# Sixty-four latent blocks of a projection: both parts of the input in one 512-column product

## Chip, cores, metric

One core of a Trainium2 chip. The metric is the device time of one execution in microseconds (us); the time before is the median of three runs. TensorE is called PE, VectorE DVE, ScalarE ACT; SyncE (SP) issues the DMAs.

## What is computed

One layer of a diffusion backbone over 256 latent tokens (`x`) and 256 context tokens, 2048 channels, in fp32. Norm and adaLN give `hn`; one input projection gives seven parts, of which a convolution branch and a recurrent branch use six:

```python
u = hn @ w_in[l] + b_in[l]
a, g, z_c, xr, z_r, gc, gr = jnp.split(u, SPLITS, axis=-1)
v = a * jax.nn.sigmoid(g)                       # conformer_branch
v = depthwise_conv(vr, p["conv_dw"], half, half)  # 31 taps, rows of 64 tokens
v = jax.nn.silu(layernorm(v + p["conv_dw_b"], p["conv_ln_g"], p["conv_ln_b"]))
y_conv = (v * jax.nn.silu(z_c)) @ p["w_conv_out"]
y_rnn = ((hf + hb) * jax.nn.silu(z_r)) @ p["w_rnn_out"]   # hf, hb: scans over xr
y = jax.nn.sigmoid(gc) * y_conv + jax.nn.sigmoid(gr) * y_rnn
x = x + gt[:, None] * (y @ p["w_o"])            # then the final RMSNorm
```

## The kernel before

Channels lie on the partitions, tokens in the free dimension. Every fp32 operand of a product is an exact pair of parts, a leading one and a remainder: the input as `xh` and `xl` (16 channel tiles, context and latents), the weights as `whi` and `wlo`. A product of the pairs is three products: `whi` with `xh`, `whi` with `xl`, `wlo` with `xh`.

After a start phase (adaLN, norms, eight xr blocks) the weights come as a stream of blocks, 128 output channels by 2048 input channels, 1 MB each. `slot` (L573) does one block: it issues the load of block s+3, and for each half of the block `block_mms` (L381) emits 24 products; then `stage_split` (L372) emits ACT's `whi` (L180) for half a block two blocks ahead and DVE's `wlo` (L185) for the half before that; then `run_deferred` (L406) runs what was put off by a number of half slots with `defer`, and `run_side` (L411) side work. For latents alone a product has 256 columns and a block is 48 products.

Side work stands in one queue: pieces with a cost in us that is written beside them (0.37 for a convolution tap). Each half slot takes pieces off the queue until half the block's budget is used up (`BUD_ZR`, `BUD_R`, `BUD`, `BUD_LN`, L26). So the program order of DVE and ACT is fixed when the program is built, and by these numbers; engines run in that order.

The order of the blocks: xr and zr in turn (zr has 16), then a and g in turn (32), zc (16), gr (16), rnn_out (16), gc (16), conv_out (16), then the output projection (w_o) in four column chunks with 512-column products. The side queue has first the recurrent branch (taps, gates on PE, scan); when it is empty, `feed` (L701) opens the memory of the second phase, and the convolution's taps come in (`conv_ops`, L647) as pairs of tiles are ready. Behind the last taps comes the LayerNorm: mean (`ln_mean`, L711), centring and squares, variance (`ln_var`, L738), `ln_rstd` (L742) and then in the side queue `ln_a` (L766: scaling on DVE, swish on ACT), `ln_b` (L770: product with the gate) and `ln_split` (L773: a leading part on ACT, a remainder on DVE), tile by tile. The sums over partitions go through PE: `ln_total` (L715) emits a product named `tot` where the program stands. Behind the last gc block everything left in the side queue is emitted at once:

```python
    while side or any(queue):
        run_side(1e9)
        run_deferred()
```

The conv_out blocks read what `ln_split` wrote. `gt_start`, the last piece of the side queue, starts a row of 64 DVE steps for adaLN's gate of the output (`gt_step`, L817), two after each gc and conv_out block and one after each half block of w_o; a chunk of 16 steps ends in a product `gps` (L833) and an ACT copy, which the evacuation of the chunk (`evac_o`, L890) needs.

Evacuation before: ACT reads the 256 columns of a block out of PSUM with bias and function in one operation (`evac_a` L688, `evac_g` L692, zc at L790; `evac_zr` L556 with two).

Of the kernel before, what the change touches and what calls it, by code (L numbers as in the profile page):

```python
# [81 lines left out]
def block_kernel(ctx, tc, xcat, xtok, fgrow, par, wada, wgt, bgt, wearly, wall, wgate, out):  # L82
# [120 lines left out]
    def ada_mms(acc, raw, rnd, n):  # L203
        # raw holds 8 // n channel tiles of 128 n columns of w_ada
# [7 lines left out]
    def ada_fin(row, part, k0, n):  # L212
        # sums of the four partial rows, channels to partitions
# [11 lines left out]
    def stat_mm(acc, x, i):  # L225
        # mean over channels: four column groups of the array take every fourth tile
# [10 lines left out]
    with ExitStack() as st:  # L237
# [28 lines left out]
        # with the tokens on the partitions, and back  # L266
# [18 lines left out]
        def normalise(ks):  # L285
# [16 lines left out]
            # partial sums, in the end where the input's first tiles were  # L302
# [69 lines left out]
    def stage_split(s, h):  # L372
        """the weights' leading parts; the remainders of the half block before"""
# [23 lines left out]
    side = deque()  # L397
# [626 lines left out]
```

## Time and profile before

| what | us |
|---|---|
| median of three runs (1145.42 to 1146.89) | 1146.66 |
| span of the profiled execution (its own time beside the runs isn't given apart) | 1142.0 |
| PE busy | 1121.5 |
| DVE busy | 924.9 |
| ACT busy | 615.1 |

The span goes from the first to the last instruction that the profile shows; a run's time has a few us more around it. Busy times overlap between engines, so they don't add up to the span. In the chain of waits every us of the span is put down to one engine: the one that the end was waiting for. A matmul's duration in the profile contains its pipeline; what one costs in a row is the distance from start to start.

### The profile page before, as it was taken

To read this page: it belongs to the slowest core of one execution; us is meant where nothing else is said; L and a number is where in the kernel's file an instruction comes from. 1 tells how busy PE (TensorE), PEld (TensorE's weight loads), DVE (VectorE), ACT (ScalarE), POOL (GpSimd) and SP (SyncE) were. 2 spreads that over 40 slices of the span, in tenths; PEclk is the share of its full clock that TensorE was granted. 3 is DMA by queue.
4 is the path that set the end of the run, shared out by engine and by line. 5 is a ranking of instruction groups with operands and counts; after the bars stand their busy time and mean duration, and the time that the engine had idled before them with its cause. 6 is when DMAs were issued, how large, how long until landed. Compare 5 with 4: busy or idle time off the path is not lost.

```text
span 1142.0 us, 20720 instructions
## 1 busy us (share of the span) xinstructions
PE 1121.5 (98%) x8316; PEld 1010.7 (88%) x8316; DVE 924.9 (81%) x1528; ACT 615.1 (54%) x838; POOL 0.2 (0%) x4
## 2 busy tenths in 40 slices
PE   6999999999999999999999999999999999999996
PEld 3777778777798989999999999999999999999885
DVE  5555588789879888899998989999985977888885
ACT  3222279777888877644454444443335854444443
POOL 0000000000000000000000000000000000000000
PEclk9999999999999999999999999999999999999999
DMA  9998444233346555465555555555554569888772
GB/s 376 400 409 324 189 134 134 102 125 125 106 141 196 160 167 164 143 209 184 185 185 171 183 183 185 175 183 178 181 188 150 169 205 324 316 310 285 268 279 93
DMA packets 67635, 233.70 MB, mean 205 GB/s; under 512 B 7505, under 2 KB 11729, under 8 KB 67153
## 3 DMA queue, kind: packets, MB, share of 16 engines
q1 hardware_dynamic: 67538, 232.37, 59.5%
q8 instruction: 65, 1.06, 0.4%
q14 instruction: 32, 0.26, 0.1%
HBM read 230.25 MB, written 2.10 MB: 203 GB/s over the span
## 4 chain that ended last, share of the span: by engine, by line
PE 98%; DVE 1%; DMA 0%; ACT 0%; issue 0%; ACTq 0%; SPq 0%; DVEq 0%
PE acc L234 72%; PE o L912 8%; PE xr L234 6%; PE gate L472 5%; PE ada L209 2%; PE part L234 2%; PE ms L228 1%; DMA hbuf<-in_xcat_dram 0%; PE tp L216 0%; PE mps L228 0%; PE gps L833 0%; PE vps L228 0%; DVE sq L259 0%; DVE wlo L171 0%; PE tot L279 0%
## 5 line engine op out<-in xcount | busy, mean ns | idle before, releaser
L234 PE MATMUL acc<-xh,whi 128*128 128x256 f32 (+1 forms) x2176 | 566.8, 296 | 0.0
L234 PE MATMUL acc<-xl,whi 128*128 128x256 f32 (+1 forms) x2176 | 552.3, 289 | 0.0
L180 ACT ACTIVATE whi<-raw 128x1024 fp32r<-128x1024 f32 x304 | 321.1, 1058 | 351.0 <-PE acc L234 277.3
L234 PEld LDWEIGHTS acc<-xh,whi 128*128 128x128 f32 x2176 | 416.7, 192 | 17.8 <-issue 9.3
L234 PEld LDWEIGHTS acc<-xl,whi 128*128 128x128 f32 x2176 | 416.9, 192 | 12.5 <-issue 7.7
L185 DVE TENSOR_TENSOR wlo<-raw,whi 128x1024 fp32r<-128x1024 f32 x304 | 371.0, 1223 | 70.0 <-ACT whi L180 66.3
L234 PE MATMUL acc<-xh,wlo 128*128 128x256 f32 (+1 forms) x2176 | 319.0, 289 | 0.0
L234 PEld LDWEIGHTS acc<-xh,wlo 128*128 128x128 f32 x2176 | 288.2, 192 | 5.0
L660 DVE SCALAR_TENSOR_TENSOR cv<-hbuf,pt,cv 128x196 f32<-128x196 f32 (+14 forms) x480 | 185.9, 451 | 13.0 <-ACT cv L651 12.6
L461 DVE SCALAR_TENSOR_TENSOR xc<-xr,pt,xc 128x510 f32<-128x510 f32 (+2 forms) x96 | 71.0, 742 | 0.2
L472 PE MATMUL gate<-xc,gw 128*128 128x512 f32 x128 | 60.0, 592 | 0.0
L820 DVE SCALAR_TENSOR_TENSOR zc<-gtraw,csil,zc 128x512 f32<-128x512 f32 x64 | 47.9, 748 | 5.4 <-DMA gtraw<-in_wgt_dram 4.7
L234 PE MATMUL xr<-xh,whi 128*128 128x512 f32 x96 | 40.4, 421 | 0.4 <-ACT xh L170 0.4
L912 PE MATMUL o<-whi,xh 128*128 128x512 f32 x128 | 40.6, 399 | 0.0
L498 DVE TENSOR_TENSOR_SCAN tr<-a,ti 128x512 f32<-128x512 f32 x32 | 39.1, 1223 | 0.7
L333 ACT ACTIVATE row<-ada 128x128 f32<-128x128 f32 (+1 forms) x22 | 7.2, 326 | 60.2 <-PE ada L209 60.2
L912 PE MATMUL o<-whi,xl 128*128 128x512 f32 x128 | 39.5, 389 | 0.0
L912 PE MATMUL o<-wlo,xh 128*128 128x512 f32 x128 | 39.4, 389 | 0.0
L234 PE MATMUL xr<-xl,whi 128*128 128x512 f32 x96 | 37.7, 392 | 0.2 <-DVE xl L171 0.2
L472 PEld LDWEIGHTS gate<-xc,gw 128*128 128x128 f32 x128 | 22.8, 189 | 17.0 <-issue 13.9
L234 PE MATMUL xr<-xh,wlo 128*128 128x512 f32 x96 | 37.4, 390 | 0.0
L209 PE MATMUL ada<-adaraw,csil 128*32 128x128 f32 (+1 forms) x704 | 32.5, 324 | 1.1 <-DVE sh L218 0.9
(169 smaller groups left out, 838.1 us busy)
## 6 DMA issues: line engine op xcount, KB each, us to landing
raw<-in_wall_dram SPq DMA_DIRECT2D x304, 512.0 KB, 3.5
adaraw<-in_wada_dram SPq DMA_DIRECT2D x64, 512.0 KB, 8.5
gtraw<-in_wgt_dram SPq DMA_DIRECT2D x32, 512.0 KB, 3.9
raw<-in_wearly_dram SPq DMA_DIRECT2D x16, 512.0 KB, 9.9
gw<-in_wgate_dram SPq DMA_DIRECT2D x32, 128.0 KB, 3.2
hbuf<-in_xcat_dram SPq DMA_DIRECT2D x2, 1024.0 KB, 7.1
cv<-in_xtok_dram SPq DMA_DIRECT2D x4, 512.0 KB, 5.8
out_dram<-cv SPq DMA_DIRECT2D x6, 256.0 KB, 2.6
```

What stands on the lines that cost most here:

```text
L180: A.activation(out=hi, in_=raw, func=AF.Copy)
L185: V.tensor_tensor(out=lo, in0=raw, in1=hi.bitcast(F32), op=SUB)
L209: PE.matmul(out=acc[g:g + 32, :w], lhsT=csil[:, k, :], rhs=raw[:, w * q:w * q + w], start=(k < 4), stop=(k >= KT - 4), tile_position=(0, g))
L228: PE.matmul(out=acc[32 * q:32 * q + 32, :], lhsT=ones[:, :32], rhs=x, start=(i < 4), stop=(i >= KT - 4), tile_position=(0, 32 * q))
L234: PE.matmul(out=acc, lhsT=w, rhs=x, start=(first and i == 0), stop=(last and i == n - 1))
L333: A.activation(out=row, in_=acc, func=AF.Copy)
L461: V.scalar_tensor_tensor(out=o, in0=i, scalar=w, in1=o, op0=MUL, op1=ADD)
L472: PE.matmul(out=acc, lhsT=u["gw"][:, c:c + 128], rhs=u["xc"], start=True, stop=True)
L498: V.tensor_tensor_scan(out=r(u["tr"]), data0=r(u["a"]), data1=r(u["ti"]), initial=0.0, op0=MUL, op1=ADD)
L660: V.scalar_tensor_tensor(out=o, in0=i, scalar=hdw[:, m * CW + j:m * CW + j + 1], in1=o, op0=MUL, op1=ADD)
L820: V.scalar_tensor_tensor(out=gt_chunk(c), in0=gt_raw[0][:, 512 * (k % 2):512 * (k % 2) + 512], scalar=csil[:, k, 0:1], in1=gt_chunk(c), op ...
L912: PE.matmul(out=acc, lhsT=y[:, k, 1, P * i:P * i + P], rhs=w[:, 512 * kk:512 * kk + 512], start=(k == 0 and w is hi and y is xh), stop=(k ...
```

## The change

The two parts of the input become one tile `xx`, in which the leading part and the remainder of a channel tile's latents lie side by side, 512 columns. In the 64 blocks zr, a, g and zc a half block is now eight products of `whi` with 512 columns, the leading part's sum in the first half of a PSUM bank and the remainder's in the second, and eight products of `wlo` with `xh` into the first half. ACT copies the second half with the bias, and half a slot later DVE adds the first half (`gather`); the function (Tanh, Silu) is an ACT operation from SBUF another half slot later, and products that follow come later still. Blocks that read the context half or come after zc are left as they were. The budgets of side work are new: 2.4 after zr (2.7 before), 2.6 in a/g while the recurrent branch runs (3.0), 2.2 after that and in zc (`BUD_H`; 2.9).

```diff
-BUD_XR, BUD_ZR, BUD_R, BUD, BUD_LN = 8.0, 2.7, 3.0, 2.9, 2.6
+BUD_XR, BUD_ZR, BUD_R, BUD_H, BUD, BUD_LN = 8.0, 2.4, 2.6, 2.2, 2.9, 2.6
...
-    xh = const.tile([P, KT, 2, T], F32R, name="xh")
-    xl = const.tile([P, KT, 2, T], F32R, name="xl")
+    xx = const.tile([P, KT, 2, 2, T], F32R, name="xx")
+    xh, xl = xx[:, :, :, 0, :], xx[:, :, :, 1, :]
...
+    def gather(t, acc, bias):
+        A.activation(out=t, in_=acc[:, 1], func=AF.Identity, bias=bias)
+        defer(0, lambda: V.tensor_tensor(out=t, in0=acc[:, 0], in1=t, op=ADD))
+
...
-        A.activation(out=tz, in_=acc, func=AF.Tanh, scale=0.5, bias=hbin[:, BZR + m:BZR + m + 1])
-        A.activation(out=zz, in_=acc, func=AF.Identity, bias=pc("b_in", BZR + m))
+        gather(zz, acc, pc("b_in", BZR + m))
+        defer(1, lambda: A.activation(out=tz, in_=zz, func=AF.Tanh, scale=0.5))
...
-        defer(0, product)
+        defer(2, product)
+
+    def pair_mms(s, acc, half):
+        hi, lo = parts.pop((s, half))
+        for kk in range(8):
+            k = 8 * half + kk
+            PE.matmul(out=acc, lhsT=hi[:, 128 * kk:128 * kk + 128], rhs=xx[:, k, 1], start=(k == 0), stop=False)
+        for kk in range(8):
+            k = 8 * half + kk
+            PE.matmul(out=acc[:, 0], lhsT=lo[:, 128 * kk:128 * kk + 128], rhs=xh[:, k, 1], start=False, stop=(k == KT - 1))
...
-            block_mms(s, view, *mov, h)
+            if mov:
+                block_mms(s, view, *mov, h)
+            else:
+                pair_mms(s, view, h)
...
-            evac_zr(b - BZR, slot(s, lat, T, BUD_ZR))
+            evac_zr(b - BZR, slot(s, None, T, BUD_ZR))
...
-        A.activation(out=av[m], in_=acc, func=AF.Identity, bias=pc("b_in", BA + m))
+        gather(av[m], acc, pc("b_in", BA + m))
...
-        A.activation(out=tg, in_=acc, func=AF.Tanh, scale=0.5, bias=hbin[:, BG + m:BG + m + 1])
-        V.scalar_tensor_tensor(out=vb[:, m], in0=tg, scalar=1.0, in1=av.pop(m), op0=ADD, op1=MUL)
-        ready.append(m)
+        gather(tg, acc, pc("b_in", BG + m))
+        defer(1, lambda: A.activation(out=tg, in_=tg, func=AF.Tanh, scale=0.5))
+
+        def product():
+            V.scalar_tensor_tensor(out=vb[:, m], in0=tg, scalar=1.0, in1=av.pop(m), op0=ADD, op1=MUL)
+            ready.append(m)
+        defer(2, product)
...
-        evac_a(m, slot(s, lat, T, BUD if tp2 else BUD_R))
+        evac_a(m, slot(s, None, T, BUD_H if tp2 else BUD_R))
...
-        acc = slot(s, lat, T, BUD)
-        A.activation(out=zc[:, m], in_=acc, func=AF.Silu, bias=pc("b_in", BZC + m))
+        acc = slot(s, None, T, BUD_H)
+        feed()
+        gather(zc[:, m], acc, pc("b_in", BZC + m))
+        defer(1, lambda m=m: A.activation(out=zc[:, m], in_=zc[:, m], func=AF.Silu))
```

Some temporary tiles get a third buffer, and `feed` runs what is deferred before it opens the second phase.

How the instructions stand, at the places of which the prediction speaks. First PE where the LayerNorm's total of the variance goes through it (`tot`, the second product of that name; `vps` sums the squares, `acc` with a number is a block). Before, between the two halves of a gc block:

```order
L228 MATMUL vps<-sq,ones 32x256 x2
...
L234 MATMUL acc_9733<-xh,wlo 128x256 x8
L717 MATMUL tot<-rstd,sel_73 128x256
L234 MATMUL acc_9733<-xh,whi 128x256
L234 MATMUL acc_9733<-xl,whi 128x256
```

Now:

```order
L229 MATMUL vps<-sq,ones 32x256 x2
L235 MATMUL acc_9485<-xx,whi 128x256 x16
L235 MATMUL acc_9485<-xx,wlo 128x256 x8
...
L743 MATMUL tot<-rstd,sel_73 128x256
L235 MATMUL acc_9646<-xx,whi 128x256 x16
L235 MATMUL acc_9646<-xx,wlo 128x256 x8
```

The block ahead of `tot` is the last gc block, `acc_9485`, both halves, and `acc_9646` is the first conv_out block (in the listing of DVE its evacuation is that of L905); before, `tot` stands within the fifth gc block, `acc_9733`, and 11 more gc blocks follow.

Second, ACT at the same place: `rstd` is the square root behind `tot`, `cv<-cv` the swish of a tile, `whi` a half block's leading part, `hbuf<-acc` the evacuation of a gc block. Before:

```order
L180 ACTIVATE whi<-raw 128x1024
L196 ACT_TABLE_LOAD
L196 ACTIVATE rstd<-var,epst 128x256
L768 ACT_TABLE_LOAD
L768 ACTIVATE cv<-cv,pt 128x256 x3
L180 ACTIVATE whi<-raw 128x1024
L768 ACTIVATE cv<-cv,pt 128x256
L863 ACTIVATE hbuf<-acc_9733,hbin 128x256
L180 ACTIVATE whi<-raw 128x1024
L768 ACTIVATE cv<-cv,pt 128x256 x2
```

and so on, one or two swishes between two `whi`. Now (`xx<-cv` is the split's copy, `xx<-p` what follows the first conv_out block):

```order
L181 ACTIVATE whi<-raw 128x1024 x2
L197 ACT_TABLE_LOAD
L197 ACTIVATE rstd<-var,epst 128x256
L794 ACT_TABLE_LOAD
L794 ACTIVATE cv<-cv,pt 128x256 x3
L893 ACTIVATE hbuf<-acc_9485,hbin 128x256
L794 ACTIVATE cv<-cv,pt 128x256 x13
L171 ACTIVATE xx<-cv 128x256 x16
L181 ACTIVATE whi<-raw 128x1024 x2
L171 ACTIVATE xx<-p_4727 128x256
```

The 16 swishes and the 16 copies stand in one piece now, with only the last gc block's evacuation among them, and the next `whi` comes behind them. DVE's scalings, products and subtractions stand in one piece in the same way.

Third, DVE in the last column chunk of w_o (`zc<-gtraw` is a gt step, `hbuf<-o` the evacuation of a chunk's row tile). Before:

```order
L896 SCALAR_TENSOR_TENSOR hbuf<-o_12056,zc 128x512
L897 TENSOR_TENSOR cv<-cv,hbuf 128x512
L899 TENSOR_TENSOR cv<-cv,zc 128x512
L901 TENSOR_TENSOR ms_11710<-ssq 128x1
L902 TENSOR_TENSOR ms_11710<-ms_11710,ssq 128x1
L185 TENSOR_TENSOR wlo<-raw,whi 128x1024 x5
L896 SCALAR_TENSOR_TENSOR hbuf<-o_12225,zc 128x512
```

Now:

```order
L932 TENSOR_TENSOR ms_10762<-ms_10762,ssq 128x1
L186 TENSOR_TENSOR wlo<-raw,whi 128x1024
L850 SCALAR_TENSOR_TENSOR zc<-gtraw,csil,zc 128x512
...
L186 TENSOR_TENSOR wlo<-raw,whi 128x1024
L850 SCALAR_TENSOR_TENSOR zc<-gtraw,csil,zc 128x512 x4
L926 SCALAR_TENSOR_TENSOR hbuf<-o_11284,zc 128x512
```

Eight gt steps (four behind a remainder each, four in a row) stand here that stood further ahead; four of them are behind the last remainder and ahead of the evacuation.

## Rows read from the trace of the kernel before

**Rows 1.** The page: busy time of the engines; the chain of waits by engine.

```profile
PE 1121.5 (98%) x8316; PEld 1010.7 (88%) x8316; DVE 924.9 (81%) x1528; ACT 615.1 (54%) x838; POOL 0.2 (0%) x4
...
PE 98%; DVE 1%; DMA 0%; ACT 0%; issue 0%; ACTq 0%; SPq 0%; DVEq 0%
```

**Rows 2.** The chain in order of time: start us, us, what, of which line.

```profile
458.53 92.15 PE acc L234 x768
...
883.75 112.31 PE acc L234 x936
...
1077.37 43.56 PE o L912 x192
1121.79 10.94 PE o L912 x48
```

**Rows 3.** Busy time by stretch: length, then PE, PEld, DVE, ACT, POOL; clock, DMA.

```profile
500.00:800.00 300.00, 300.00 (x2489) 296.73 (x2488) 275.69 (x525) 133.30 (x161) 0.00 (x0) 1.00 0.56 182
```

**Rows 4.** Groups by line and form: busy us, mean ns of one, for 256 columns.

```profile
L690 ACT ACTIVATE av<-acc,pt 128x256 f32<-128x256 f32 x16 | 7.4, 463 | 0.0
...
L875 DVE SCALAR_TENSOR_TENSOR hbuf<-hbuf,acc 128x256 f32<-128x256 f32 x16 | 6.7, 419 | 0.3
```

**Rows 5.** DVE in order of time, LayerNorm before conv_out: start us, us, what.

```profile
883.78 0.42 DVE L718 COPY var<-tot 128x256 f32<-128x256 f32 x1 [1.95 <-PE tot L717]
...
888.86 0.76 DVE L767 TENSOR_TENSOR cv<-cv,rstd 128x256 f32<-128x256 f32 x2
889.96 0.43 DVE L771 TENSOR_TENSOR cv<-cv,zc 128x256 f32<-128x256 f32 x1 [0.34 <-ACT cv L768]
...
892.10 0.42 DVE L767 TENSOR_TENSOR cv<-cv,rstd 128x256 f32<-128x256 f32 x1
892.44 0.42 DVE L771 TENSOR_TENSOR cv<-cv,zc 128x256 f32<-128x256 f32 x1
```

**Rows 6.** DVE in order of time, an a/g block with the convolution's taps.

```profile
496.02 1.22 DVE L185 TENSOR_TENSOR wlo<-raw,whi 128x1024 fp32r<-128x1024 f32 x1
497.16 1.46 DVE L660 SCALAR_TENSOR_TENSOR cv<-hbuf,pt,cv 128x204 f32<-128x204 f32 x4
...
503.66 0.42 DVE L698 SCALAR_TENSOR_TENSOR hbuf<-tg,av 128x256 f32<-128x256 f32 x1
503.99 1.23 DVE L185 TENSOR_TENSOR wlo<-raw,whi 128x1024 fp32r<-128x1024 f32 x1
```

**Rows 7.** ACT in order of time, the same LayerNorm: swish and split copies.

```profile
889.32 1.09 ACT L768 ACTIVATE cv<-cv,pt 128x256 f32<-128x256 f32 x2 [2.69 <-DVE cv L767]
...
915.50 1.32 ACT L170 ACTIVATE xh<-cv 128x256 fp32r<-128x256 f32 x4
```

**Rows 8.** DVE in order of time, split subtractions and the first gt steps.

```profile
915.94 1.43 DVE L171 TENSOR_TENSOR xl<-cv,xh 128x256 fp32r<-128x256 f32 x4 [0.65 <-ACT xh L170]
...
935.92 1.54 DVE L820 SCALAR_TENSOR_TENSOR zc<-gtraw,csil,zc 128x512 f32<-128x512 f32 x2 [4.66 <-DMA gtraw<-in_wgt_dram]
```

**Rows 9.** Busy time by stretch at the end, columns as in group 3.

```profile
1130.00:1133.00 3.00, 2.71 (x12) 1.90 (x11) 1.93 (x8) 1.42 (x3) 0.00 (x0) 1.00 0.18 69
...
1136.00:1138.00 2.00, 0.00 (x0) 0.00 (x0) 1.22 (x5) 1.33 (x2) 0.00 (x0) 0.79 0.10 38
1138.00:1140.00 2.00, 0.00 (x0) 0.00 (x0) 0.00 (x0) 0.00 (x0) 0.00 (x0) 0.50 1.01 380
```

**Rows 10.** The page: DMA issues, KB each, us from issue to landing.

```profile
raw<-in_wall_dram SPq DMA_DIRECT2D x304, 512.0 KB, 3.5
```

**Rows 11.** DVE and ACT in order of time, the last column chunk.

```profile
1116.36 4.63 DVE L185 TENSOR_TENSOR wlo<-raw,whi 128x1024 fp32r<-128x1024 f32 x4
1122.12 1.23 DVE L185 TENSOR_TENSOR wlo<-raw,whi 128x1024 fp32r<-128x1024 f32 x1 [1.14 <-ACT whi L180]
1127.38 0.69 DVE L896 SCALAR_TENSOR_TENSOR hbuf<-o,zc 128x512 f32<-128x512 f32 x1 [4.03 <-PE o L912]
...
1122.00 0.58 ACT L834 ACTIVATE zc<-gps 128x512 f32<-128x512 f32 x1
```

More of the change, by code (lines that the diff above doesn't have):

```diff
@@ L291, in normalise @@
             for k in ks:
-                split(xh[:, k].rearrange("p s t -> p (s t)"), xl[:, k].rearrange("p s t -> p (s t)"), xin(k))
+                split(xh[:, k], xl[:, k], xin(k).rearrange("p (s t) -> p s t", s=2))
         def products(m, ks, ws):
@@ L510, in r_sum @@
         else:
-            hs = rp.tile([P, T], F32, tag="hs", name="hs", bufs=2)
+            hs = rp.tile([P, T], F32, tag="hs", name="hs", bufs=3)
             V.tensor_tensor(out=hs, in0=f[:, T:], in1=b[:, :T], op=ADD)
@@ L553, in r_tick @@
         side.append((0.0, lambda: emitted.__setitem__(0, t)))
+    def gather(t, acc, bias):
+        A.activation(out=t, in_=acc[:, 1], func=AF.Identity, bias=bias)
+        defer(0, lambda: V.tensor_tensor(out=t, in0=acc[:, 0], in1=t, op=ADD))
     def evac_zr(m, acc):
-        tz = rp.tile([P, T], F32, tag="tz", name="tz", bufs=2)
+        tz = rp.tile([P, T], F32, tag="tz", name="tz", bufs=3)
         direct = m not in have_h
-        zz = hbuf[:, m] if direct else rp.tile([P, T], F32, tag="hs", name="zz", bufs=2)
-        A.activation(out=tz, in_=acc, func=AF.Tanh, scale=0.5, bias=hbin[:, BZR + m:BZR + m + 1])
-        A.activation(out=zz, in_=acc, func=AF.Identity, bias=pc("b_in", BZR + m))
+        zz = hbuf[:, m] if direct else rp.tile([P, T], F32, tag="hs", name="zz", bufs=3)
+        gather(zz, acc, pc("b_in", BZR + m))
+        defer(1, lambda: A.activation(out=tz, in_=zz, func=AF.Tanh, scale=0.5))
         if direct:
@@ L570, in product @@
                 hz_product(m, zz)
-        defer(0, product)
+        defer(2, product)
[7 more added lines that the diff above has]
+            PE.matmul(out=acc[:, 0], lhsT=lo[:, 128 * kk:128 * kk + 128], rhs=xh[:, k, 1], start=False, stop=(k == KT - 1))
     def slot(s, mov, N, budget):
         acc = psum(f"acc{s}")
-        view = acc[:, :N] if N == T else acc.rearrange("p (s t) -> p s t", s=2)
+        view = acc[:, :N] if N == T and mov else acc.rearrange("p (s t) -> p s t", s=2)
         stage_load(s + 3)
         for h in range(2):
-            block_mms(s, view, *mov, h)
+            if mov:
+                block_mms(s, view, *mov, h)
+            else:
+                pair_mms(s, view, h)
             stage_split(s + 2, h)
@@ L582, in slot @@
             run_side(budget / 2)
-        return acc if N == 512 else acc[:, :N]
+        return acc if N == 512 else acc[:, :N] if mov else view
     s = 0
@@ L684, in vtmp @@
         if tp2 is None:
-            return rp.tile([P, T], F32, tag="tz", name=name, bufs=2)
+            return rp.tile([P, T], F32, tag="tz", name=name, bufs=3)
         return tp2.tile([P, T], F32, tag="ag", name=name, bufs=3)
@@ L696, in evac_g @@
         tg = vtmp("tg")
-        A.activation(out=tg, in_=acc, func=AF.Tanh, scale=0.5, bias=hbin[:, BG + m:BG + m + 1])
-        V.scalar_tensor_tensor(out=vb[:, m], in0=tg, scalar=1.0, in1=av.pop(m), op0=ADD, op1=MUL)
-        ready.append(m)
-    def feed():
-        if tp2 is None and not side and not av and not any(queue):
-            open_ph2()
+        gather(tg, acc, pc("b_in", BG + m))
[4 more added lines that the diff above has]
+        defer(2, product)
+    def feed():
+        if tp2 is None and not side:
+            while any(queue):
+                run_deferred()
+            if not side and not av:
+                open_ph2()
         while tp2 is not None and len(ready) > 1:
@@ L777, in block_kernel @@
     for m in range(KT):
-        evac_a(m, slot(s, lat, T, BUD if tp2 else BUD_R))
+        evac_a(m, slot(s, None, T, BUD_H if tp2 else BUD_R))
         s += 1
-        evac_g(m, slot(s, lat, T, BUD if tp2 else BUD_R))
+        evac_g(m, slot(s, None, T, BUD_H if tp2 else BUD_R))
         feed()
@@ L788, in block_kernel, with zc_done @@
     for m in range(KT):
-        acc = slot(s, lat, T, BUD)
-        A.activation(out=zc[:, m], in_=acc, func=AF.Silu, bias=pc("b_in", BZC + m))
+        acc = slot(s, None, T, BUD_H)
+        feed()
+        gather(zc[:, m], acc, pc("b_in", BZC + m))
+        defer(1, lambda m=m: A.activation(out=zc[:, m], in_=zc[:, m], func=AF.Silu))
         s += 1
-    ln["zc"] = True
-    ln_gates()
+    def zc_done():
+        ln["zc"] = True
+        ln_gates()
+    defer(2, zc_done)
     xo = cv.rearrange("p k t -> p (k t)")
```

## Prediction

> **What bounds the kernel now.** The page comes first: TensorE (PE) is busy for 1121.5 of 1142.0 us and the chain of waits gives it 98% of the span [rows 1]. So a gain must come out of PE's own time, and any hole in PE's row is a loss; the other engines count only where PE ends up waiting for them. The page gives a span of 1142.0 us and no own time of that execution; the three runs have a median of 1146.66 us, 4.7 us more, and I carry those 4.7 us along unchanged.
>
> Second, the chain in order of time, for the price of a product. 768 products of 256 columns take 92.15 us, 120.0 ns each; 192 products of 512 columns in the output projection take 43.56 us, 226.9 ns each [rows 2]. Twice the columns cost less than twice the time: a product has a part of some 13 ns that doesn't grow with its columns.
>
> Third, busy time by stage, for the cover. Between 500 and 800 us VectorE (DVE) works 275.7 of 300 us [rows 3]. It is the engine with least room, and the change gives it more to do.
>
> **The change, part by part.** *Products.* In 64 blocks (16 zr, 32 a/g, 16 zc) 32 products of 256 columns with the leading weights become 16 of 512; the 16 with the remainders stay. A pair cost 2 x 120.0 = 240.0 ns and now costs 226.9: 13.1 ns less, x 16 x 64 = **13.4 us off PE**, 5.76 to 5.55 us a block. The nearest bad case is the 48 products of 512 columns in 10.94 us [rows 2], 227.9 ns each, 12.4 us in all; I take 13.4, since that row is short and includes its own end. The Trainium skill, page "TensorE: Matmul & The Clock Gate", section "Back-to-back issue gap", speaks against the change: there a product at full clock takes its columns at 2.4 GHz and 2.5 ns, so a pair would save 2.5 ns, 2.6 us in all, and the sum below would end at 1164.7. The trace disagrees, with 13 ns instead of 2.5, so the sum goes by the trace.
>
> *Evacuation.* A bank now holds two halves. ACT copies one half with the bias, DVE adds the other, and the nonlinearity follows from SBUF: 64 DVE additions, 32 more ACT operations. No addition like it is in the trace; a DVE operation on 256 columns with a PSUM input has 419 ns, an ACT one 463 [rows 4]. In a row, DVE's operations of this size start some 0.34 us apart [rows 5], so 64 x 0.34 = 21.8 us of DVE. I cost it at nothing on PE, as long as DVE fits. Before, half a block on DVE was a remainder of weights (1.14 us from start to start) and four taps (1.4 us), with the gating product of 0.34 every fourth half [rows 6]: 5.3 of 5.76 us a block. Now a block has 2 x 1.14 for weights, 0.34 for the addition, 0.17 for gating, and, with the budget cut from 2.9 to 2.2 us (six taps of 0.37), 6 x 0.36 = 2.2 of taps: 5.0 of 5.55 us. So it fits, and it fits because the budget was cut. Without that cover, at the old budget, DVE would need 5.6 against PE's 5.55.
>
> *The budgets* are where the cost returns. Side work is placed in program order by budget, not by when DVE is idle. The convolution's taps begin four blocks later (the recurrent branch's budget fell too), run at 2.2 instead of 2.9 a block up to the zc blocks' end, and so the LayerNorm behind them comes 11 blocks later. The order listings show where that puts it: in the kernel before, the total of the variance (the second `tot`) stands in the middle of the fifth gc block, with 11 gc blocks behind it to cover all that follows. Now it stands behind the last gc block, and the next thing on PE is the first conv_out block, whose moving operand is what the LayerNorm is still to produce. Scaling, swish and gate of 16 tiles and 16 splits stand in one piece on DVE and ACT; PE has nothing left to do.
>
> I work out that hole from the same steps before, by the clock of that execution. At 883.75 PE went on with its next block [rows 2]; that is the instant at which it would now begin conv_out.
> - Copy of the total at 883.78, square root, reciprocal, Newton step: first scaling at 888.86 [rows 5]. 5.1 us.
> - Per tile a DVE multiplication, an ACT swish and a DVE product with the gate, the next tile's multiplication between them. Tile 0 took 1.10 us from the first start to the product's start; DVE's starts are 0.34 us apart [rows 5], a swish takes about 0.55 to 0.6 [rows 7]. If DVE alone sets the pace, a tile costs 0.67 us; if every tile waits out its swish in full, 1.10. With one multiplication ahead, multiplications are 1.10 + 0.34 us apart every second tile, 0.72 a tile, near DVE's own pace, since only two engines alternate. The last product starts at 888.86 + 15 x 0.72 + 1.10 = 900.8 and ends at 901.1; 0.2 us for the last gc block's own ACT operation in between.
> - ACT's copies take 0.33 us a tile [rows 7], DVE's subtractions 0.36 [rows 8]; PE starts on the first tile's copy at about 901.7. A tile's two products take PE 0.24 us, so the first half block goes at DVE's pace, 8 x 0.36 + 0.96 for the remainders; the second half has its tiles in time, 2.9 us. Block done at some 908.3, against 883.75 + 5.76 = 889.5.
>
> **A hole of 18.8 us**; 18.0 at 0.67 us a tile, 24.5 at 1.10.
>
> *The clock.* Behind PE's last product the granted clock reads 0.79 in 1136 to 1138 us and 0.50 in 1138 to 1140 [rows 9], the level of 1.2 GHz. After such a hole PE may come back at that level. No row of this case shows the way back up. At nothing it costs 0; if the whole block ran at the low level, its 48 products would take 107 ns more each (256 columns at 1.2 instead of 2.4 GHz, an estimate), 5.1 us, of which about a quarter hides behind the splits: 4. I take 0.7, near the low end, because in the first microseconds DVE sets the pace anyway. The page of the Trainium skill named above, section "Part 1: The HAM clock gate (the "warmup" mystery)", says the half rate is what an idle array falls back to and that work releases it; the rows at the end agree with its first half.
>
> *The rest of the path.* The gt steps (0.74 us each on DVE, two in 1.54 [rows 8]) can't start before the hole is over, so eight that stood in gc blocks move back. Their loads move with them: on SP's queue the first two and a row of biases, which waits for DVE's clearing of the chunks behind the splits, now stand ahead of the weights of the fourth conv_out block; a load takes 3.5 us to land [rows 10] and those weights are wanted three blocks later, so I cost that at nothing. conv_out and the output projection take two a block as before, and the last eight now stand in the last column chunk, four of them behind the last weights' remainder. Before, DVE had its last five remainders there, four in 4.63 us, then waited 4.03 us for PE [rows 11]. With eight steps more (5.7 us) the room is gone: the last step ends near 1116.4 + 5 x 1.14 + 8 x 0.72 = 1127.9, and the sum gps, which PE now runs between the last two row tiles, waits for it. Before, DVE took that row tile over from PE at 1127.38 [rows 11]; without gps ahead of it PE is there some 0.5 us earlier, at 1126.9. So 1.0 us of waiting, and 0.4 because the copy of gps, 0.58 us on ACT [rows 11], makes the first row tile's work on DVE run into the second's: **1.4 us**, between 0 (DVE's steps get ahead in the longer hole) and 2.5 (all of the copy and of gps on the path).
>
> Sum: 1146.66 - 13.4 + 18.8 + 0.7 + 1.4 = 1154.2; the span 1149.5.
>
> **The rivals.** (1) *The hole is covered.* The conv_out blocks would have to start within 12 us of the total. Then the saving shows: 1146.66 - 13.4 + 1.4 = 1134.7. It decides at the first split: DVE's own work up to there is 5.1 + 16 x 0.67 = 15.8 us, and nothing of it may start before the total. For it speaks only that DVE and ACT were mostly idle just before. 0.05; another 0.04 that the pieces are all at their low ends and the time comes out within 0.2% of before.
> (2) *The hole is deeper.* Tiles in full alternation (24.5), or the low clock for a block and more (4): 1159 to 1163. The wait of 0.34 us at tile 0 [rows 5] speaks for some of it; the overlap in the order speaks against. 0.13.
> (3) *DVE becomes the bound* in the 64 blocks, the additions having been costed too low: each 0.1 us a block over PE's 5.55 costs 6.4 us. Half the addition unabsorbed, 0.17 a block, gives 1165. The 0.55 us of room speaks against it. 0.03.
> (4) *Pairs save nothing*, if 512 columns spread over two halves took as long as two products, 240 ns: 1154.2 + 13.4 = 1167.6. The skill's rule above would be near it. Both lengths stand in the same trace at the same clock, 226.9 against 120.0 [rows 2], which speaks against it. 0.02.
> That the products aren't merged is excluded: in the order of the changed kernel eight products of 128x512 stand in each half of these blocks.
>
> **How the numbers follow.** The forecast has 0.73, at 1154.2. Its own range, 18.0 to 20.5 us of hole, 12.4 to 13.4 saved, 0 to 2 of clock, 0 to 2.5 at the end, is about 1151.3 to 1158.5; to leave out no more than 2 in 10 the range takes in the milder part of (2) and some room below: 1149 to 1161. About 0.2% (2.3 us) is what a measurement of this kernel can tell from no change. Faster by more than that is rival 1 alone, 0.05; within it, its weaker form, 0.04; slower, all the rest, 0.91.
>
> **What would show it.** Products of 512 columns 227 ns apart and blocks of 5.55 us between about 375 and 650 us; PE without a gap there. One gap in PE's row of 17 to 18 us before the first conv_out block, ended by DVE's and ACT's split, around 936 us. In the gap, one piece of scalings and products on DVE, 11 to 12 us long. The granted clock below 1 in the slice behind it. A wait of PE for the last gps. I am wrong if PE shows no gap of over 12 us there, if pairs take more than 235 ns, or if DVE leaves gaps in PE's row in the a, g and zc blocks.

## The result, and the profile after

The changed kernel takes 1159.8 us (median of four runs, 1156.67 to 1160.2), the kernel before 1146.04 beside it; the ratio is 1.0117 [1.0104, 1.0129]. It is slower, as forecast; the time is 5.6 us above the forecast of 1154.2 and inside the range.

The page of the changed kernel has the same form as before [rows 1]: PE nearly full, now with fewer and longer products.

```profile
span 1157.7 us, 18763 instructions
PE 1118.0 (97%) x7292; PEld 961.8 (83%) x7292; DVE 946.3 (82%) x1592; ACT 624.5 (54%) x870; POOL 0.2 (0%) x4
...
PE 95%; DVE 2%; ACT 1%; DMA 1%; issue 0%; ACTq 0%; SPq 0%; DVEq 0%
```

A table by stretch says where the time went. The ends of a stretch are the first product of a block on PE, the first evacuation of rnn_out on DVE, and the first and last product of the output projection (first and last starts of these lines):

| us | to first block | blocks to rnn_out | rnn_out to w_o | w_o |
|---|---|---|---|---|
| before | 151.8 | 613.0 | 278.4 | 89.0 |
| after | 154.5 | 601.3 | 298.6 | 93.6 |
| difference | +2.7 | -11.7 | +20.2 | +4.5 |

The sum is 15.7, the difference of the spans. The first column isn't the change: over the eleven profiles of the experiments it lies between 151.7 and 155.2 us with the same start phase. It goes with the granted clock (the clock that the throttle lets TensorE have, as a share of 2.4 GHz) in that phase. Busy time by stretch (columns as in [rows 3]; the last three numbers are granted clock, DMA share, GB/s), before and after:

```profile
10.00:40.00 30.00, 25.95 (x288) 17.40 (x285) 18.15 (x42) 9.14 (x18) 0.00 (x0) 1.00 1.02 409
10.00:40.00 30.00, 26.19 (x274) 17.13 (x271) 16.32 (x38) 8.28 (x17) 0.00 (x0) 0.89 1.02 409
```

In the five profiles of before and the experiments where it reads 1.00 here, the first block starts at 151.7 to 152.4; at 0.94 (three) at 152.6 to 153.4, at 0.83 to 0.89 (four, and the changed kernel) at 154.5 to 155.2. So one execution of the same kernel can be some 3 us longer than another. The other three columns make 13.0 us, against 13.8 between the medians.

PE in order of time, the blocks of a and g. A half is eight pairs and eight remainders:

```profile
501.08 2.00 PE L584 MATMUL acc<-xx,whi 128*128 128x512 f32 x8
502.93 1.12 PE L587 MATMUL acc<-xx,wlo 128*128 128x256 f32 x8
503.88 2.00 PE L584 MATMUL acc<-xx,whi 128*128 128x512 f32 x8
505.72 1.11 PE L587 MATMUL acc<-xx,wlo 128*128 128x256 f32 x8
506.67 2.00 PE L584 MATMUL acc<-xx,whi 128*128 128x512 f32 x8
```

From start to start a half takes 2.79 us, a block 5.59 (5.76 before), with no gap. Then the hole (PE idle ahead of the first conv_out block), PE in the same view:

```profile
941.29 0.59 PE L743 MATMUL tot<-rstd,sel 128*128 128x256 f32 x2
959.26 4.06 PE L235 MATMUL acc<-xx,whi 128*128 128x256 f32 x16 [17.38 <-ACT xx L171]
963.12 1.36 PE L235 MATMUL acc<-xx,wlo 128*128 128x256 f32 x8
...
967.20 1.00 PE L235 MATMUL acc<-xx,whi 128*128 128x256 f32 x7
```

DVE in order of time, what fills it: copy of the total, the chain to the first scaling, products in turn with scalings, and the splits (before: [rows 5], [rows 8]):

```profile
941.92 0.42 DVE L744 COPY var<-tot 128x256 f32<-128x256 f32 x1 [1.95 <-PE tot L743]
...
946.99 0.76 DVE L793 TENSOR_TENSOR cv<-cv,rstd 128x256 f32<-128x256 f32 x2
948.08 0.43 DVE L797 TENSOR_TENSOR cv<-cv,zc 128x256 f32<-128x256 f32 x1 [0.33 <-ACT cv L794]
...
958.94 0.42 DVE L797 TENSOR_TENSOR cv<-cv,zc 128x256 f32<-128x256 f32 x1 [0.34 <-ACT cv L794]
959.28 5.45 DVE L172 TENSOR_TENSOR xx<-cv,xx 128x256 fp32r<-128x256 f32 x16
```

The tail (the last column chunk of w_o), as the chain of waits has it (start us, us, what): DVE's last steps, the landing of the last load, two more steps, then gps and the second row tile.

```profile
1134.32 0.76 DVE zc L850
1135.10 3.41 DMA gtraw<-in_wgt_dram
...
1138.60 0.76 DVE zc L850
...
1140.19 1.16 PE gps L863 x2
1141.35 7.06 PE o L942 x24
```

The waits there, DVE's and PE's, in their rows in order of time:

```profile
1138.60 1.54 DVE L850 SCALAR_TENSOR_TENSOR zc<-gtraw,csil,zc 128x512 f32<-128x512 f32 x2 [0.94 <-DMA gtraw<-in_wgt_dram]
1140.19 1.16 PE L863 MATMUL gps<-zc,unit 128*128 128x512 f32 x2 [2.15 <-DVE zc L850]
```

And the clock, busy time by stretch (columns as above):

```profile
950.00:962.00 12.00, 2.74 (x11) 2.54 (x12) 11.57 (x34) 10.60 (x24) 0.00 (x0) 0.50 0.00 1
962.00:964.00 2.00, 2.00 (x13) 2.00 (x12) 2.00 (x8) 2.00 (x7) 0.00 (x0) 0.58 0.00 0
964.00:967.00 3.00, 3.00 (x28) 3.00 (x27) 2.78 (x8) 1.27 (x2) 0.00 (x0) 1.00 0.00 0
...
1141.00:1144.00 3.00, 3.00 (x8) 2.29 (x7) 1.91 (x3) 1.13 (x2) 0.00 (x0) 0.53 0.00 0
...
1146.00:1148.00 2.00, 2.00 (x10) 1.66 (x9) 0.60 (x2) 1.06 (x2) 0.00 (x0) 1.00 0.45 170
```

PE starts again at 959.26 at the level of 1.2 GHz (granted clock 0.50) and is at 2.4 (1.00) from 964 on. In the tail it falls to the low level again, behind a wait of only 2.15 us.

### The profile page after: what moved, and what is told of

It reads as the page before. It is cut to its first block, busy times and chain, and to the rows that moved or that the text cites. A ratio compares the mean times of both kernels' runs of the same rounds, so it can differ in the third digit from the quotient of the medians.

```text
span 1157.7 us, 18763 instructions
## 1 busy us (share of the span) xinstructions
PE 1118.0 (97%) x7292; PEld 961.8 (83%) x7292; DVE 946.3 (82%) x1592; ACT 624.5 (54%) x870; POOL 0.2 (0%) x4
## 4 chain that ended last, share of the span: by engine, by line
PE 95%; DVE 2%; ACT 1%; DMA 1%; issue 0%; ACTq 0%; SPq 0%; DVEq 0%
PE acc L235 40%; PE acc L584 20%; PE acc L587 11%; PE o L942 7%; PE xr L235 6%; PE gate L473 5%; PE ada L210 2%; PE part L235 2%; PE ms L229 1%; DMA hbuf<-in_xcat_dram 0%; PE tp L217 0%; DVE cv L797 0%; DVE cv L793 0%; PE mps L229 0%; DVE zc L850 0%
## 5 line engine op out<-in xcount | busy, mean ns | idle before, releaser
L181 ACT ACTIVATE whi<-raw 128x1024 fp32r<-128x1024 f32 x304 | 321.0, 1058 | 338.8 <-PE acc L235 180.8
L235 PE MATMUL acc<-xx,whi 128*128 128x256 f32 (+1 forms) x2304 | 335.4, 298 | 17.4 <-ACT xx L171 17.4
L235 PEld LDWEIGHTS acc<-xx,whi 128*128 128x128 f32 x2304 | 304.3, 192 | 37.2 <-ACT xx L171 17.8
L584 PE MATMUL acc<-xx,whi 128*128 128x512 f32 x1024 | 265.1, 401 | 0.0
L584 PEld LDWEIGHTS acc<-xx,whi 128*128 128x128 f32 x1024 | 185.7, 189 | 44.0 <-issue 9.3
L679 DVE SCALAR_TENSOR_TENSOR cv<-hbuf,pt,cv 128x196 f32<-128x196 f32 (+14 forms) x480 | 186.5, 446 | 12.4 <-ACT cv L670 12.0
L235 PE MATMUL acc<-xx,wlo 128*128 128x256 f32 (+1 forms) x1152 | 175.5, 295 | 0.0
L235 PEld LDWEIGHTS acc<-xx,wlo 128*128 128x128 f32 x1152 | 156.5, 192 | 5.0
L587 PEld LDWEIGHTS acc<-xx,wlo 128*128 128x128 f32 x1024 | 139.7, 190 | 10.1
L587 PE MATMUL acc<-xx,wlo 128*128 128x256 f32 x1024 | 142.8, 282 | 0.0
L942 PE MATMUL o<-whi,xx 128*128 128x512 f32 x256 | 71.0, 400 | 0.0
L235 PE MATMUL xr<-xx,whi 128*128 128x512 f32 x192 | 63.6, 412 | 0.4 <-ACT xx L171 0.4
L942 PEld LDWEIGHTS o<-whi,xx 128*128 128x128 f32 x256 | 48.9, 191 | 11.5 <-issue 1.4
L942 PE MATMUL o<-wlo,xx 128*128 128x512 f32 x128 | 39.9, 393 | 0.0
```

What stands on the lines that cost most here:

```text
L181: A.activation(out=hi, in_=raw, func=AF.Copy)
L235: PE.matmul(out=acc, lhsT=w, rhs=x, start=(first and i == 0), stop=(last and i == n - 1))
L584: PE.matmul(out=acc, lhsT=hi[:, 128 * kk:128 * kk + 128], rhs=xx[:, k, 1], start=(k == 0), stop=False)
L587: PE.matmul(out=acc[:, 0], lhsT=lo[:, 128 * kk:128 * kk + 128], rhs=xh[:, k, 1], start=False, stop=(k == KT - 1))
L679: V.scalar_tensor_tensor(out=o, in0=i, scalar=hdw[:, m * CW + j:m * CW + j + 1], in1=o, op0=MUL, op1=ADD)
L942: PE.matmul(out=acc, lhsT=y[:, k, 1, P * i:P * i + P], rhs=w[:, 512 * kk:512 * kk + 512], start=(k == 0 and w is hi and y is xh), stop=(k ...
```

## The experiments

Theory A: the pairs (one product of 512 columns in place of two of 256) gain, and the lower budgets lose more than that, by the hole and the tail. Its rivals differ by experiment. The same stretches of all runs; the ratio is to the kernel before, run beside each:

| us | median | ratio | to rnn_out | to w_o | w_o |
|---|---|---|---|---|---|
| e1 pairs, old budgets | 1133.04 | 0.9898 [0.9883, 0.9913] | 602.3 | 278.4 | 89.0 |
| e2 no pairs, low budgets | 1170.59 | 1.0216 [1.0199, 1.0233] | 612.1 | 298.8 | 93.4 |
| e3 later budget raised | 1146.21 | 1.0012 [1.0000, 1.0024] | 601.3 | 285.7 | 93.7 |
| e4 three gt steps | 1164.89 | 1.0171 [1.0155, 1.0186] | 601.3 | 305.0 | 93.7 |
| e5 last steps left out | 1153.15 | 1.0081 [1.0059, 1.0103] | 601.3 | 298.3 | 89.5 |
| e6 products in the hole | 1156.23 | 1.0095 [1.0080, 1.0110] | 601.3 | 297.6 | 91.8 |
| e7 flat 512 | 1135.30 | 0.9914 [0.9898, 0.9930] | 602.3 | 278.4 | 89.0 |
| e8 pairs in gr, gc too | 1129.02 | 0.9860 [0.9846, 0.9875] | 600.2 | 275.0 | 89.0 |
| e9 budget 3.6 | 1147.98 | 1.0018 [1.0009, 1.0028] | 616.4 | 277.7 | 88.1 |
| e10 alternating | 1133.90 | 0.9903 [0.9885, 0.9920] | 602.6 | 278.4 | 89.0 |
| e11 pairs in all 128 | 1136.78 | 0.9925 [0.9905, 0.9944] | 604.5 | 275.3 | 92.7 |

Some medians miss the ranges on record, by up to 1.9 us: those of e1, e5 and e6 lie below theory A's, that of e2 above, that of e4 above its rival's. For the first four the start phase is part of that (first block at 151.9, 151.7, 153.4 and 155.2, in the changed kernel at 154.5), so what follows goes by the stretches.

**e1, the pairs without the new budgets.**

```diff
-BUD_XR, BUD_ZR, BUD_R, BUD_H, BUD, BUD_LN = 8.0, 2.4, 2.6, 2.2, 2.9, 2.6
+BUD_XR, BUD_ZR, BUD_R, BUD_H, BUD, BUD_LN = 8.0, 2.7, 3.0, 2.9, 2.9, 2.6
```

> The changed kernel with the budgets of the kernel before (2.7, 3.0, 2.9, 2.9 in zc); pair products and the evacuation through DVE's addition stay. Theory A (the time was lost by the budgets alone, and the pairs gain): the LayerNorm's total stands in the fifth gc block again, so no hole of 17 us ahead of conv_out and no wait for the last gps; the 64 blocks give some 11 to 13 us, so 1133.5 to 1138 against 1146, depending on whether the 2.7 us that the first weight block came later in the changed kernel's profile (154.67 against 152.00 us) come back. Theory B (VectorE becomes the bound at the old budgets, 5.6 us of work for a block of 5.55): gaps on PE in the a, g and zc blocks that VectorE's remainder ends, and at least 2 to 6 us of the gain lost: 1138 to 1143. Theory C (pairs save nothing): 1146.

Hole and tail are gone, the last two stretches are those of the kernel before to 0.1 us, and 1133.04 is 12.5 us faster than before. Theory B fell: PE waits for no remainder of DVE's. But DVE has nothing to spare. Busy time by stretch (columns as above), 500 to 640 us:

```profile
500.00:560.00 60.00, 60.00 (x345) 52.32 (x344) 60.00 (x122) 30.32 (x41) 0.00 (x0) 1.00 0.58 186
560.00:640.00 80.00, 80.00 (x461) 69.51 (x460) 80.00 (x160) 42.74 (x61) 0.00 (x0) 1.00 0.59 193
```

DVE (third) is busy for all 140 us, and so is PE (first). A block's weights are split two blocks ahead, so DVE may be late by some us before PE sees it; this lead wasn't varied.

**e2, the new budgets without the pairs**, in the kernel before.

```diff
-BUD_XR, BUD_ZR, BUD_R, BUD, BUD_LN = 8.0, 2.7, 3.0, 2.9, 2.6
+BUD_XR, BUD_ZR, BUD_R, BUD_H, BUD, BUD_LN = 8.0, 2.4, 2.6, 2.2, 2.9, 2.6
...
-        evac_a(m, slot(s, lat, T, BUD if tp2 else BUD_R))
+        evac_a(m, slot(s, lat, T, BUD_H if tp2 else BUD_R))
```

and the same in g and zc.

> The kernel before with the new, lower budgets alone (2.4, 2.6, and 2.2 in a/g of the second phase and in zc); products and evacuation as before. Theory A (hole and tail come from the budgets alone): the total stands behind the last gc block as in the changed kernel; hole of 19.5 us, tail of 1.4 to 4.3, so 1146 + 21 to 24 = 1167 to 1170; PE idle 17 to 18 us ahead of the first conv_out block. Rival (the hole comes from the gathered evacuation, which puts nonlinearities later): no gap over 5 us, 1146 to 1149.

1170.59: hole and tail to 0.2 us as in the changed kernel, without a single pair. The page's group of the leading products has the whole gap, 17.4 us, ended by the split:

```profile
L234 PE MATMUL acc<-xh,whi 128*128 128x256 f32 (+1 forms) x2176 | 568.1, 296 | 17.4 <-ACT xh L170 17.4
```

The four kernels (before, e1, e2, changed) make a square: pairs give 10.8 us on either budget (613.0 to 602.3; 612.1 to 601.3), the budgets cost 20.2 to 20.4 and 4.4 to 4.5 in the later stretches with or without pairs, and give 0.9 before rnn_out.

**e3, more side work later.** `BUD_LN` 2.6 to 3.6 in the changed kernel.

> The changed kernel (low budgets in the 64 blocks) with 3.6 instead of 2.6 us of side work for each gc block, so that the LayerNorm's total of the variance stands in the fourth block from the end instead of behind the last. Theory A (the hole is what is left of the LayerNorm's chain when conv_out is due, so some 3.5 blocks of 5.76 us cover as much of it as VectorE can do beside the weights): in 20 us VectorE finishes the first 5.1 us of the chain and some 8.5 of the 10.7 us of scalings and products; 3 to 6 us of idle PE are left of 17.4, 1144 to 1147.5, the tail unchanged at some 4 us more than before. Rival (budget 3.6 makes VectorE late for the weights in the gc blocks, 2.28 + 3.3 + the gt steps for 5.76, or the pieces queue in an order that leaves the splits last): the hole falls by less than 10 us or PE waits in the gc blocks, over 1149.

In PE's view the gap is 4.65 us, ended by the split:

```profile
946.85 0.44 PE L235 MATMUL acc<-xx,whi 128*128 128x256 f32 x1 [4.65 <-ACT xx L171]
```

So 12.7 of 17.4 us are covered by three and a half blocks, as theory A has it; tail unchanged (93.7).

**e4, three gt steps a conv_out block.** `GTN` 2 to 3 in the changed kernel.

> The changed kernel with three gt steps after a conv_out block instead of two (GTN 3), so that all gt steps are done before the last column chunk of the output projection. Theory A (the tail's 4.3 us more than before are the wait for the last gps, with the low clock behind it): no gap on PE in the last chunk, 3 to 4.5 us less than the changed kernel, 1155 to 1157. Rival (the tail is longer for another reason, or VectorE and the loads can't take three steps, 5.6 us of work on VectorE in a block of 5.76 and loads that take 3.5 us with two buffers): less than 1.5 us gained or time lost in conv_out, 1158 to 1163.

The rival. The gt steps came in time, and the kernel lost 5 us. Waits of PE (us in total, times, longest), two pieces of the chain in conv_out, and the loads of weights in the conv_out blocks, here (960 to 1058 us) and in the changed kernel (960 to 1054; count, KB each, median us from issue to landing):

```profile
PE o L942 <- DVE wlo L186: 3.8, 4, 1.3
PE acc L235 <- DVE wlo L186: 3.2, 5, 1.1
```

```profile
976.52 7.55 DMA raw<-in_wall_dram
...
1060.37 6.18 DMA gtraw<-in_wgt_dram
```

```profile
raw<-in_wall_dram SPq DMA_DIRECT2D x30, 512.0 KB, 6.8
raw<-in_wall_dram SPq DMA_DIRECT2D x32, 512.0 KB, 5.5
```

The loads of weights on the path take 7.2 to 8.2 us here. Their median over these blocks is 6.8, in the changed kernel 5.5 (the 3.5 of [rows 10] is the median of the whole kernel): the six gt steps of two blocks bring three loads of 512 KB beside the four of weights, where four steps bring two. Between 955 and 1065 us the chain gives the loads of weights 35%, those of gt 11% and the gt steps themselves 18%; how much of the loss is the loads and how much DVE's third step isn't parted.

**e5, the last gt steps left out.**

```diff
-        gt_todo.extend(range(4 * KT))
+        gt_todo.extend(range(4 * KT - 8))
...
-            if n // 2 + GTB < 32:
+            if n // 2 + GTB < 28:
...
-        if k == KT - 1:
+        if k == KT - 1 or n == 4 * KT - 9:
```

> The changed kernel without the last eight of the 64 gt steps and their four loads (the gate of the last column chunk lacks half of its sum); product gps, its copy and all else stay. Theory A (the tail's extra time is PE's wait for these steps and their loads, and the low clock behind that wait): PE doesn't wait for gps, the 24 products behind it take 5.5 us instead of some 7.1, and from the first to the last product of the output projection it takes 89.0 to 89.5 us as in the kernel before, not 93.5; 1155 to 1156. Rival 1 (only the wait counts, the low clock comes back after the first hole in any case): 2.2 us less, 91.3. Rival 2 (gps between the two row tiles costs by itself): over 92.

w_o takes 89.5 us, theory A's value. But the edit does one thing more: gps comes earlier, ahead of both row tiles as in the kernel before, as the chain shows.

```profile
1129.46 0.86 PE gps L863 x2
1130.32 10.94 PE o L942 x48
```

So it shows that the late steps are the tail's cause, and doesn't by itself part wait, clock and the place of gps. e6 does that. The 0.5 us over the kernel before are no loss: in the kernels with low budgets six gps products stand in w_o, before it was four; one pair has moved here from conv_out.

**e6, PE kept busy in the hole.**

```diff
+    keep = psum("keep")[:, :T]
+    for n in range(136):
+        PE.matmul(out=keep, lhsT=parts[s, 0][0][:, 128 * (n % 8):128 * (n % 8) + 128], rhs=xh[:, n % KT, 1],
+                  start=(n == 0), stop=(n == 135))
```

> The changed kernel with 136 more products of 256 columns between the LayerNorm's total and the first conv_out block, into a bank that nothing reads; they take 136 x 0.12 = 16.3 us of a gap of 17.4. If the low clock after the gap costs something (theory A): granted clock 1.00 when conv_out starts, the time from the total's copy to the end of the first conv_out block falls from 25.3 us by 0.7 to 1.5 us, and the whole kernel by as much, 1158 to 1159. Rival (the pace of the first block is VectorE's splits alone, and the clock costs nothing): within 0.3 us of the same stretch; and if the added products delay the splits or the weights, longer.

PE in order of time:

```profile
940.14 0.59 PE L743 MATMUL tot<-rstd,sel 128*128 128x256 f32 x2
940.38 16.65 PE L902 MATMUL keep<-xx,whi 128*128 128x256 f32 x136
958.12 3.21 PE L235 MATMUL acc<-xx,whi 128*128 128x256 f32 x16 [1.09 <-ACT xx L171]
...
965.00 2.08 PE L235 MATMUL acc<-xx,whi 128*128 128x256 f32 x16
```

From `tot` to the second block 24.86 us, 25.91 in the changed kernel: the low clock cost **1.05 us**. The splits come at the same time with or without PE's work. (The 25.3 of the expectation count from the total's copy.) The tail changed too, which I hadn't expected: PE waits 2.0 us for gps, but the granted clock reads 1.00 throughout and the 24 products behind take 5.50 us instead of 7.06 (chain, then busy time by stretch).

```profile
1138.97 5.50 PE o L947 x24
```

```profile
1138.00:1142.00 4.00, 4.00 (x16) 2.96 (x17) 2.23 (x4) 1.32 (x3) 0.00 (x0) 1.00 0.00 0
```

So of the tail's 4.5 us some 1.6 are low clock, 2.0 to 2.2 the wait, and 0.8 is left (91.8 - 89.0 - 2.0): 0.5 the pair of gps that moved here (e5), some 0.3 at the restart, not parted further. The rest of e6's gain over the changed kernel is its earlier start (153.4 against 154.5). Why the clock holds behind one wait of 2 us and falls behind another isn't settled, and the wait's length alone doesn't decide it: in e2, behind a wait of 2.01 us, it fell as in the changed kernel (24 products in 7.10), in e6, behind 2.00, it held.

**e7, one dimension of 512** instead of two of 256, in input and bank of the pairs (`rearrange("p s t -> p (s t)")`), on e1.

> The changed kernel with the old budgets, and in the pair products the two halves of input and bank written as one dimension of 512 instead of 2 x 256. In the run with the old budgets eight pair products take 1.84 us, 230 ns each, against 226.9 in the output projection, whose operands have one dimension. Theory A (the two dimensions cost those 3 ns): 227 ns, eight in 1.815 us, 64 blocks 3.2 us shorter, 1130. Rival (the 3 ns come from elsewhere, such as the change between 512 and 256 columns, or the two forms are the same instruction): still 1.84, 1133.

```profile
501.62 2.00 PE L584 MATMUL acc<-xx,whi 128*128 128x512 f32 x8
503.46 1.11 PE L587 MATMUL acc<-xx,wlo 128*128 128x256 f32 x8
```

Still 1.84 us for eight (501.62 to 503.46): the rival. But the test is empty on the side of the input: the trace records the moving operand of the pairs as one dimension of 512 in e1 already, as in e7 and in the output projection, since the two halves lie side by side. What it was meant to test stands elsewhere in the same traces. In the xr blocks the operand is recorded as two dimensions of 256, and 16 products take 3.62 us, 226 ns each (e1, PE in order of time):

```profile
151.86 3.79 PE L235 MATMUL acc<-xx,whi 128*128 128x512 f32 x16
155.48 1.98 PE L235 MATMUL acc<-xx,wlo 128*128 128x512 f32 x8
```

So two dimensions of the input cost nothing. The median lies 2.3 us above e1's with the same stretches from the first block on: its first block came at 155.0 instead of 151.9, with a granted clock of 0.83 between 10 and 40 us.

**e10, the order in a block.** On e1, in the second half of each block:

```diff
-        for kk in range(8):
+        for w in ((hi, lo), (lo, hi))[half]:
```

with the pairs' loop or the remainders' inside, by `w`.

> The changed kernel with the old budgets, and in the second half of each of the 64 blocks the remainders' eight products come ahead of the eight pair products, so that 16 products of 512 columns stand in a row across two blocks. In the run with the old budgets the first five of eight pair products start 232 ns apart and the last three 226.7. Theory A (a change from 256 to 512 columns costs some 25 ns once, spread over the next five products): 16 in a row take 16 x 226.9 + 25 = 3.655 us instead of 3.68, 64 x 25 ns = 1.6 us less in all, 1131.4. Rival (the 25 ns belong to each group of eight, such as to the wait for its weights): 3.68, no difference from 1133.

```profile
506.10 3.82 PE L586 MATMUL acc<-xx,whi 128*128 128x512 f32 x16
509.75 2.08 PE L588 MATMUL acc<-xx,wlo 128*128 128x256 f32 x16
511.66 3.82 PE L586 MATMUL acc<-xx,whi 128*128 128x512 f32 x16
```

Sixteen pairs in 3.65 us (506.10 to 509.75), a block in 5.565: theory A, in the products. Some 25 ns are paid at each change from 256 to 512 columns. The 1.3 us that this is worth in 64 blocks are given back: PE now waits 1.2 us for a remainder, which it wants 1.8 us earlier from a DVE without any slack. The time stays that of e1.

**e9, the budget too high.** `BUD_H` 3.6 on e1.

> The changed kernel with the old budgets, except 3.6 instead of 2.9 in the a, g blocks of the second phase and in zc. VectorE's work in such a block is then 2 x 1.14 + 0.34 + 0.17 + 3.5 = 6.3 us against 5.59 of PE. Theory A (rival 3 of the prediction: above PE's time a block, PE pays the difference once the lead of two blocks is used up): 0.7 us x some 30 blocks less a lead of some 5 to 8 us, so 12 to 16 us slower than with the old budgets, 1143 to 1150, PE waiting for VectorE's remainder. Rival (the taps come in pairs of tiles only when a and g of both are done, so the queue of side work runs empty and the budget isn't used): within 4 us of the old budgets, 1133 to 1137.

14.9 us slower than e1, 14.1 of it between the first block and rnn_out. Busy time by stretch and PE's wait:

```profile
500.00:640.00 140.00, 136.29 (x749) 111.13 (x748) 140.00 (x295) 65.58 (x90) 0.00 (x0) 1.00 0.53 169
```

```profile
PE acc L587 <- DVE wlo L186: 4.0, 12, 0.7
```

DVE (third) is full again, and now PE gets through 749 products in these 140 us, where in e1 it was 806 (345 + 461 in the rows above): 7%, some 10 us. The waits listed are only 4.0 us of that: PE counts as busy for 136.29 of the 140 us with fewer products in them, so its busy time doesn't show the loss. So the room on DVE that the budget had to respect is real, and it ends between 2.9 and 3.6.

**e8 and e11, more pairs.** On e1, gr and gc as pairs, evacuated like zc (e8); rnn_out and conv_out too, with e10's order and 2.5 of side work in rnn_out (e11).

```diff
-        acc = slot(s, lat, T, BUD)
-        A.activation(out=p2[:, m], in_=acc, func=AF.Tanh, scale=0.5, bias=hbin[:, BGR + m:BGR + m + 1])
+        acc = slot(s, None, T, BUD)
+        gather(p2[:, m], acc, pc("b_in", BGR + m))
+        defer(1, lambda m=m: A.activation(out=p2[:, m], in_=p2[:, m], func=AF.Tanh, scale=0.5))
```

and gc in the same way.

> The changed kernel with the old budgets, and pair products with the gathered evacuation in the 32 blocks of gr and gc as well. Theory A (a pair saves 10 ns wherever VectorE has the room, as measured in the 64 blocks): 32 x 16 x 10 ns = 5.1 us less than with the 64 blocks alone, 1127.5 to 1130, no new gap on PE. Rival (VectorE, which the trace with the old budgets shows busy all the time between 500 and 640 us, has no room for 32 more additions, or the LayerNorm's own work in the gc blocks comes later): PE waits for VectorE's remainder and at least half of the gain is lost, 1130.5 or more.

> Pair products with the gathered evacuation in all 128 blocks of one half (gr, gc, rnn_out and conv_out too), in the alternating order, old budgets, 2.5 in the rnn_out blocks. Theory A (a pair saves 10 ns wherever VectorE has the room): 5.1 us less than with pairs in gr and gc added, less 1 to 3 from the order, 1121 to 1125. Rival (in rnn_out and conv_out VectorE has no room for the addition, 2.28 + 0.34 + 0.36 to 1.06 + 2.5 side work or 1.5 of gt steps a block of 5.59): PE waits for VectorE's remainder, 1127 or more.

e8 is the fastest, 1129.02, 16.2 us less than before, with no new wait of PE. e11 is slower than e8 by 7.8, the rival (it has e10's order and another budget too, so the extra blocks aren't its only difference):

```profile
PE acc L588 <- DVE wlo L186: 8.6, 7, 2.2
...
PE o L954 <- DVE wlo L186: 2.2, 2, 1.2
```

## Why the prediction was right or wrong

- **The hole: right, with its mechanism.** Forecast 18.8 + 0.7. The second conv_out block began at 967.20; without a hole it would have been 941.89 + 5.76 = 947.65, with the end of tot, just ahead of the copy, as the instant at which PE goes on, as the prediction had it. That is 19.55 us, of which e6 puts 1.05 to the clock and 18.5 to the chain. The instant is a small misreading: 883.75 is where the chain has tot's end, and PE's row has the next product at 883.40, 0.25 us behind tot's first. Counted so, the hole is 19.9. Copy to first scaling 5.07 (5.1), multiplications and products 0.72 us a tile (946.99 to 958.94), PE's gap 17.38 (17 to 18). e2 shows that the budgets alone make it.
- **The clock behind the hole: right** in size, 1.05 for 0.7, within 0 to 4. The Trainium skill, page "TensorE: Matmul & The Clock Gate", section "Part 1: The HAM clock gate (the "warmup" mystery)", says that idling drops the rate to half and work releases it; the rows now agree with both halves, 0.50 in 950 to 962 us and 1.00 from 964.
- **The pairs: right in kind, the term mis-sized.** "13.1 ns less, x 16 x 64 = 13.4 us off PE", low end 12.4; measured 10.8, below it. A pair takes 230 ns, not 226.9: the price came from a row of 192 products all of 512 columns, and here each group of eight stands behind products of 256. The first five then start 232 ns apart, the last three 226.7, and e10 halves the loss by halving the changes. 1024 x 10 ns = 10.2, and the remainders are some 5 ns a group of eight faster (0.955 us instead of 0.96). By the formula that the prediction weighed, which the Trainium skill, page "TensorE: Matmul & The Clock Gate", section "Back-to-back issue gap", gives for the gap of a product by itself, a pair would save 2.5 ns and all of them, by estimate, 2.6 us; no run is near it. The prediction's sum with that formula should read 1165.0, not 1164.7.
- **DVE fits "because the budget was cut": wrong as a condition.** e1 shows that it fits at the old budget too, with nothing to spare, 140 of 140 us busy; the prediction's 5.6 against 5.55 us (5.59 as it turned out) was an even balance, and a lead of two blocks stands behind it. The warning was sound for a higher budget: at 3.6 (e9) it costs 14 us. Since the cut was not needed, neither was the loss by hole and tail.
- **The tail: the step that failed.** Forecast 1.4, bounds 0 to 2.5; measured 4.5, of which 0.5 is the pair of gps that only moved here. Two things were left out. The sentence "a load takes 3.5 us to land [rows 10] ... so I cost that at nothing" spoke of the weights only: the last gt load can be issued only when a step has freed one of two buffers, and lands 3.41 us later, 0.94 us after DVE was ready (1137.66 to 1138.60). PE was there 0.3 us sooner than I had put it, too, and a wait of 1.0 became 2.15. And a wait of PE was priced at its length alone: the clock fell behind it, 1.6 us more on the last 24 products. The 0.4 for the copy of gps didn't come: from the last product's start to the end of the span it is 9.7 us before and after.
- **Sum.** With the measured terms -10.8 + 19.55 + 4.5 - 0.9 + 0.65 = +13.0, where I had +7.5; the tail makes 3.1 of the 5.5 us, the pairs 2.6. The last two terms are in good part work that changed its stretch: four of the mean's 32 sums (20 stood ahead of rnn_out before, 16 now) and the 0.36 us of the instant above. That the time came within the range is luck: the bounds of the terms add up to 1151.3 and 1159.3 (not 1158.5, as written), and 1159.8 lies above them, in the room left for a deeper hole, which didn't come. The 4.7 us between span and median were mostly that profile's start phase at a granted clock of 1.00: later runs lie 1.8 us above their spans.

## What to carry to other kernels

Price an edit to a static schedule by where its last piece lands, not by whether each block still fits: here a budget cut by up to 0.7 us in a block moved a chain of 16 us behind its last cover and cost twice what the products saved. Run such an edit once with the old budgets before cutting them; an engine that is 100% busy next to the bottleneck need not be late yet, if it works blocks ahead (e1). A wait of the bottleneck can cost more than its length, by what the clock loses behind it, and the last load that waits for a buffer can set the end of a chain, as in the tail. Before two profiles are compared, compare the granted clock in a stretch that the edit doesn't touch.

## What was not expected

A change from 256 to 512 columns cost some 25 ns, spread over the next five products (e10); it isn't the input's two dimensions (the xr rows under e7), and what it is stays open. The granted clock fell to the low level behind waits of 2.15 us in the changed kernel and 2.01 in e2, and not behind one of 2.00 in e6; in the start phase it fell in eight of the thirteen profiles. Loads of 512 KB in the conv_out blocks landed after a median of 6.8 us instead of 5.5 when three others, not two, stood beside every four (e4).
